# Two FFN pairs by seven block products, with the sums on VectorE, and transposes moved from TensorE to DMAs

## The chip, the cores and the metric

The kernel runs on one core of a Trainium2 chip. The core has five engines with a queue of instructions each: TensorE (PE in the profile; PEld is its weight load), VectorE (DVE), ScalarE (ACT), GpSimd (POOL) and SyncE (SP, which here only issues DMAs). They run side by side and meet at semaphores. The metric is the device time of one execution in microseconds (us); less is better.

## The reference, cut to what matters

It is one layer of a decoder, on 256 tokens of width 1024:

```
h    = rmsnorm(x);  u = h @ W_in        # columns: rnn_x | rnn_gate | q | k | v | two gates
A    = gelu(rnn_gate) * rg_lru(causal_dwconv4(rnn_x))
B    = causal attention of q, k, v      # 8 heads x 128; q and k normalised per head
y    = sigmoid(g_A) * (A @ P_A) + sigmoid(g_B) * (B @ P_B)
x    = x + y @ W_out
h    = rmsnorm(x)
x    = x + (gelu(causal_dwconv3(h @ W_up)) * (h @ W_gate)) @ W_down     # 2816 channels
```

Everything is fp32.

## The kernel before, in words

**Tiles and splits.** An fp32 product is made of three matmuls of fp32r operands (`mm3`): high by high, high by low, low by high, where high is the operand rounded to fp32r and low the rest. Weights come in chunks of 128x2048 (1 MB), each by one DMA of SP's queue into a tile `raw`; ScalarE makes `hi` by a cast, VectorE makes `lo` by a subtraction (`split_part`), and TensorE reads both. There are three `raw`, four `hi`, three `lo`. Activations are split by `split2` in the same way. TensorE's results go to eight PSUM banks, four in pool A and four in pool B.

**Units.** A unit of TensorE works off one or two chunks: `rx` (rnn_x), `rg` (rnn_gate), `k`, `q`, `v`, `ri` (the LRU's two small products), `ga` and `gb` (gates), `pr` and `pa` (P_A and P_B), `yo` (W_out), and in the FFN `up` and `gt` for five pairs of chunks (512 channels each, pairs 0 to 4), `last` for the eleventh chunk, and eleven `dn` (W_down, all added up in four banks `acc`). A unit of one chunk is 24 matmuls of 128x512. Between the units stand the heads' small products: scores `s`, transposed probabilities `pt`, outputs `o`.

**Turns.** A result that stands by tokens and is wanted by channels is turned by `turn`: a stream transpose of 32x32 blocks by VectorE, four DMAs to DRAM that reorder the blocks, one DMA back. TensorE transposes (three a head in `att_t`, 16 in `m_t` for the gated sum, 16 for `h2`) do the same through PSUM.

**FFN.** For each pair, `pair_up` copies the turned `up` into order (2 copies by VectorE), does the three-tap convolution (`conv3`: for each of four blocks one ScalarE activation and two VectorE multiply-adds of 128x255 and 128x254), then gelu; `pair_gate` multiplies with the turned `gt` and splits into `fah` and `fal`, which `dn` reads.

**LRU.** `lru_a` to `lru_d`, for each half of the channels: a product by VectorE (`rt` times the decay), tanh, exp and square of 128x1024 by ScalarE, a square root with its own ScalarE table, products and a scan by VectorE.

**The order.** Nothing is scheduled on the chip: the operations are recorded (all at line 296, `Later`), and `ORDER`, a table of numbers, says in which order they are issued. An engine works through its own row in that order. `preload_act_table(AF.Exp)` is such an operation: it loads a ScalarE table early.

Of the kernel before, what the change touches and what calls it, by code (L numbers as in the profile page):

```python
# [32 lines left out]
KEPT = {"upd": 2, "gtd": 2, "u": 1, "c": 2, "ah": 3, "al": 3, "s": 1}
UNITS = ("rx0 rx1 rx2 rx3 rg0 rg1 rg2 rg3 k0 k1 k2 k3 ri0 q0 q1 ri1 ga0 ga1 q2 q3 v0 v1 ga2 ga3 v2 v3 gb0 "
         "gb1 gb2 gb3 pr0 pr1 pr2 pr3 pa0 pa1 pa2 pa3")
AFTER = {
    "rx0.0": "s4 stats",
    "rg0.0": "ev0",
    "rg0.3": "ev1",
    "rg1.1": "rx0",  # L40
    "rg1.2": "s5 rx1",
    "rg1.3": "s6 ge0",
    "rg2.1": "xo0",
    "rg3.0": "rgr0",
    "rg3.1": "conv0",
    "rg3.2": "xo1",
    "rg3.3": "s7 ge1",
    "k0.0": "s8 s9",
    "k0.2": "rgr1 conv1",
    "k1.2": "s10 s11",  # L50
    "k1.3": "s12",
    "k2.2": "s13",
    "k2.3": "split0 decay",
    "k3.0": "gelu1 conv2 conv3 split1",
    "k3.3": "s14",
    "ri0.0": "s15",
    "ri0.2": "krs0 ks0",
    "q0.3": "krs1",
    "q1.2": "ks1",
    "q1.3": "s16 rk1",  # L60
    "ri1.3": "rk0",
    "ga0.1": "rq0",
    "ga1.1": "s17 Tk0",
    "q2.0": "s18",
    "q3.0": "s19",
    "q3.2": "Tq0",
    "v0.0": "s20",
    "v1.0": "Tk1",
    "v1.1": "qrs0",
    "v1.2": "S3 s21",  # L70
    "ga2.0": "S2",
    "ga2.1": "rq1 S1 Tq1",
    "ga2.2": "s22 S0 P3",
    "ga2.3": "s23",
    "ga3.0": "s24 s25 la0 la1",
    "ga3.1": "lb1",
    "ga3.2": "lc1 P1 lb0",
    "ga3.3": "s26",
    "v2.1": "P0 qrs1 S4",
    "v2.2": "O3 s27 s28",  # L80
    "v2.3": "ld1",
    "v3.2": "S5",
    "gb0.0": "P2",
    "gb0.1": "s29",
    "gb1.0": "gelu0 P4",
    "gb1.3": "s30 S6",
    "gb2.1": "S7",
    "gb2.2": "O2 lc0",
    "gb2.3": "O1 s31 s32 ld0",
    "gb3.0": "ya0",  # L90
    "gb3.1": "P5 ys0",
    "gb3.2": "O4",
    "pr0.0": "P7 sb0 s33",
    "pr0.2": "sa1 ya1",
    "pr0.3": "ys1",
    "pr1.0": "O5",
    "pr1.1": "s34",
    "pr1.2": "sa0",
    "pr1.3": "s35",
    "pr2.0": "P6",  # L100
    "pr2.1": "s36",
    "pr2.2": "O6",
    "pr2.3": "O0",
    "pr3.0": "s37",
    "pr3.3": "sb1",
    "pa1.0": "O7",
    "pa2.1": "m0",
    "pa3.2": "s38",
    "wo.0": "s39 m1",
    "wo.4": "m2",  # L110
    "wo.5": "s40",
    "wo.6": "m3",
    "wo.12": "n00",
    "wo.13": "n10",
    "wo.14": "s41",
    "up00.0": "s42 n01",
    "up00.2": "n11",
    "gt00.0": "s43",
    "gt00.3": "s44",
    "up01.0": "stats2",  # L120
    "up01.3": "s45 s46",
    "gt01.2": "s47",
    "up10.0": "ur0 s48",
    "up10.1": "s49",
    "up11.0": "s50",
    "up11.2": "fu0",
    "gt10.0": "s51",
    "gt10.1": "s52 gr0",
    "gt11.1": "ur1",
    "gt11.2": "s53",  # L130
    "up20.1": "fg0",
    "up21.1": "gr1",
    "up21.3": "s54",
    "gt20.2": "fu1",
    "gt21.0": "s55",
    "dn0.0": "fg1",
    "dn1.1": "gr2",
    "dn1.3": "s56",
    "up30.3": "s57 s58",
    "up31.0": "s59",  # L140
    "up31.3": "s60 ur2",
    "gt31.1": "ur3 s61",
    "gt31.2": "fu2",
    "gt31.3": "fu3 s62",
    "dn2.2": "fg2 s63 s64",
    "dn3.0": "s65",
    "up40.0": "gr3",
    "up41.3": "s66",
# [1041 lines left out]
```

## Time and profile before

| | us |
|---|---|
| median of three runs (433.44 to 434.73) | 434.29 |
| profiled execution, first to last instruction | 432.3 |
| TensorE busy in it | 427.6 (99%) |
| VectorE busy | 324.5 (75%) |
| ScalarE busy | 271.2 (63%) |
| TensorE's granted clock | 1.000 |

The profiled execution is known by its span alone; the median of the runs is 2.0 us above it, which is what lies around the first and the last instruction. Busy time of one instruction includes the overlap with the next one: where durations are added up, the distance from start to start is used, and it is read from the timeline. A matmul of 128x512 is shown with some 0.39 us, but the next one starts 0.227 us later.

### The profile page before, as it was taken

How to read it: one execution, taken by the hardware profiler on the slowest of the kernel's cores; microseconds unless marked ns; L12 is line 12 of the kernel's file. 1: busy time of each engine (PE TensorE's matmuls, PEld its weight loads, DVE VectorE, ACT ScalarE, POOL GpSimd, SP SyncE). 2: the span in 40 equal slices, each digit the busy share in tenths (PEclk: the TensorE clock that was granted, in tenths of full speed). 3: DMA queues.
4: the chain of work that ended last, by engine and by line, in shares of the span. 5: the costliest groups of instructions: out<-in, count | busy, mean ns of one | idle time of the engine just before them, and what ended most of it. 6: DMA issues, size and time to landing. Idle time of an engine off the chain costs nothing.

```text
span 432.3 us, 5409 instructions
## 1 busy us (share of the span) xinstructions
PE 427.6 (99%) x1992; PEld 357.3 (83%) x1992; DVE 324.5 (75%) x417; ACT 271.2 (63%) x307; POOL 51.9 (12%) x101
## 2 busy tenths in 40 slices
PE   9999999999999999999999999999999999999996
PEld 8888888888887888888888888888888888888885
DVE  4867499899898999865666796587888667769633
ACT  5687596886999998853241364468566556456510
POOL 0022483567160000000000000000000000000000
PEclk9999999999999999999999999999999999999999
DMA  7997945999991844474453556898888688788402
GB/s 253 395 394 256 339 169 149 295 314 335 368 313 38 284 142 149 130 238 134 181 194 116 176 203 207 299 325 253 284 265 313 237 270 262 243 286 293 152 0 97
DMA packets 33833, 101.09 MB, mean 234 GB/s; under 512 B 3216, under 2 KB 14096, under 8 KB 30352
## 3 DMA queue, kind: packets, MB, share of 16 engines
...
q10 hardware_dynamic: 144, 0.00, 0.0%
...
## 4 chain that ended last, share of the span: by engine, by line
PE 87%; DMA 5%; ACT 3%; DVE 2%; issue 2%; SPq 0%; ACTq 0%; DVEq 0%
PE acc L296 14%; PE up L296 13%; PE gt L296 13%; PE rx L296 5%; PE gb L296 5%; PE pr L296 5%; PE yo L296 5%; PE pa L296 5%; PE k L296 5%; PE rg L296 5%; DMA qm<-qd 3%; PE q L296 3%; PE last L296 3%; PE v L296 2%; DMA raw<-in_win_fm 2%
## 5 line engine op out<-in xcount | busy, mean ns | idle before, releaser
L296 DVE TENSOR_TENSOR lo<-raw,hi 128x2048 fp32r<-128x2048 f32 (+1 forms) x72 | 160.3, 2227 | 40.1 <-PE gt L296 10.5
L296 ACT CAST hi<-raw 128x2048 fp32r<-128x2048 f32 (+1 forms) x69 | 128.3, 1862 | 49.7 <-PE gt L296 11.8
L296 PE MATMUL up<-hi,h2h 128*128 128x512 f32 x80 | 31.3, 391 | 0.0
L296 PE MATMUL up<-hi,h2l 128*128 128x512 f32 x80 | 31.2, 389 | 0.0
L296 PE MATMUL up<-lo,h2h 128*128 128x512 f32 x80 | 31.1, 389 | 0.0
L296 PE MATMUL gt<-hi,h2h 128*128 128x512 f32 x80 | 31.1, 389 | 0.0
L296 PE MATMUL gt<-lo,h2h 128*128 128x512 f32 x80 | 31.1, 389 | 0.0
L296 PE MATMUL gt<-hi,h2l 128*128 128x512 f32 x80 | 31.1, 389 | 0.0
L296 PE MATMUL acc<-hi,fah 128*128 128x512 f32 x80 | 31.1, 389 | 0.0
L296 PE MATMUL acc<-lo,fah 128*128 128x512 f32 x80 | 31.1, 389 | 0.0
L296 PE MATMUL acc<-hi,fal 128*128 128x512 f32 x80 | 31.1, 389 | 0.0
L296 POOL TENSOR_TENSOR rsq<-rsq 128x8 f32<-128x8 f32 x32 | 19.2, 600 | 28.6 <-DVE rsq L296 26.3
L296 ACT ACT_TABLE_LOAD x15 | 19.2, 1283 | 1.4 <-PEq L1180 1.2
L296 DVE SCALAR_TENSOR_TENSOR fc<-fu,pv,fc 128x255 f32<-128x255 f32 (+1 forms) x40 | 17.3, 477 | 2.1 <-ACT fc L296 2.1
L296 ACT ACTIVATE fc<-fu,pv 128x256 f32<-128x256 f32 x20 | 10.8, 593 | 11.1 <-DVE fu L296 11.1
L296 PEld LDWEIGHTS up<-hi,h2l 128*128 128x128 f32 x80 | 15.0, 188 | 3.2
L296 PEld LDWEIGHTS acc<-lo,fah 128*128 128x128 f32 x80 | 15.0, 188 | 3.1
L296 PEld LDWEIGHTS acc<-hi,fal 128*128 128x128 f32 x80 | 15.0, 188 | 3.1
L296 PEld LDWEIGHTS gt<-hi,h2l 128*128 128x128 f32 x80 | 15.0, 188 | 3.1
L296 PEld LDWEIGHTS gt<-lo,h2h 128*128 128x128 f32 x80 | 15.0, 188 | 3.1
L296 PEld LDWEIGHTS gt<-hi,h2h 128*128 128x128 f32 x80 | 15.0, 188 | 3.1
L296 PEld LDWEIGHTS acc<-hi,fah 128*128 128x128 f32 x80 | 15.0, 188 | 3.1
...
## 6 DMA issues: line engine op xcount, KB each, us to landing
...
```

What stands on the lines that cost most here:

```text
L296: getattr(engine, name)(*map(real, a), **{n: real(v) for n, v in k.items()})
```

## The change

- **Pairs 2 and 4** (`ffn_group`, `group`). The four products of a pair (two halves of the tokens, two of the outputs: up and gate, each over two halves of the 1024 inputs) are a 2x2 block product. It is computed with seven block products in place of eight, of 12 matmuls each. The four weight tiles are called `x`, `y`, `w`, `z`; VectorE adds them up in place (`SUMS = "vvvv"`) to the operands `t1`, `t2`, `t4`, `t3`, and `b00`, `b10`, `b11` are split as they are. Four sums of `h` (`forms`: `R1`, `S2`, `S3`, `S4`) are the other operands. The outputs `fs0` and `fs1` are put together from the banks `a`, `b`, `c`, `d` by ScalarE and VectorE.
- **Probabilities** are turned by VectorE and DMAs (`turn` with three blocks; four writes of 48 KB, one read a head), not by TensorE.
- **Half the gated sum** (`MT = {0: True}`) goes by `turn`, the other half stays on TensorE.
- **FFN taps** (`taps`): twelve ScalarE activations a pair that read the turned tile directly, and two VectorE additions of 4x255 and 4x254.
- **LRU**: the decay is folded into tanh and exp as a per-channel scale (8 of 128x256 a half in place of 2 of 128x1024 and a VectorE product).
- **Buffers**: `raw` 5, `hi` 4, `lo` 4, 19 half tiles in place of 23, all eight banks in one pool; the residual is written to DRAM after the second norm and loaded again at the end. Three casts that VectorE did go back to ScalarE.
- **The order** is a new table.

```diff
-HALVES, SMALLS, WARM, RAWS = 23, 10, 11, 3
-DVE_HI = (39, 42, 43)
+HALVES, SMALLS, WARM = 19, 10, 11
+BUFS = {"raw": 5, "hi": 4, "lo": 4}
+SUMS = "vvvv"
+OPTS = "cdy"
+PLAN = """
+rx rg0 rg1 rg2 rg3 decay k0 k1 k2 k3 q0 q1 q2 q3 ri0 v0 v1:3 S3 P3 v1 ga0:1 S2 P2 ga0:1 S1 P1 ga0:1 S0 P0 ga0 ri1 ga1 v2:2 S4 P4 v2 v3:2 S5 P5 v3 O3 ga2:2 O2 ga2 ga3:1 S6 P6 ga3 gb0:1 S7 P7 gb0:1 O1 gb0 O0 gb1 O4 gb2 gb3 ya0 ya1 pr0 pr1:1 O5 pr1 pr2:2 O6
...
 ORDER = """
-0-2 +1 3-4 +1 5 +1 6 +1 8 +1 7 +1 9 +1 11 +2 10 25 +1 12 30 +1 26-27 +1 14 +1 28 33 +1 29 +1 13 31 +2 32 +2 34 +2
...
+0 2 1 3 +3 5 +4 6 +3 7 +1 8 10 9 11-13 15 14 132 18 24 17 29 26 25 28 +1 27 +3 32 30 +3 31 +2 33 +8 34 +7 36 35 +2 38
...
     def att_t(h):
-        sm = heads[h]
-        ps = bank(f"pt{h}")
...
+        turn(f"pm{h}", small(f"pd{h}", 384), probs[h], 3, probs[h])
+        a = small(f"ph{h}", 384, F32R), small(f"pl{h}", 384, F32R)
+        split2(*a, probs[h])
...
+    def group(name, a, src, rs, nrs, out0, out1, cols=True):
...
+        product(ps["a"], a["a00"], part("b00", x), True)
+        nc.scalar.activation(o[1][0], ps["a"], AF.Copy, scale=r[0])
+        nc.scalar.activation(o[0][1], ps["a"], AF.Copy, scale=r[1])
+        yield
+        add("1", x, y, src[0][1])
+        product(ps["c"], a["R1"], part("t1", x), True)
+        nc.scalar.activation(o[1][1], ps["c"], AF.Copy, scale=nrs[:, 1:2])
+        yield
+        product(ps["a"], a["a01"], part("b10", w), False)
+        nc.scalar.activation(o[0][0], ps["a"], AF.Copy, scale=r[0])
+        yield
+        product(ps["c"], a["S4"], part("b11", z), False)
+        yield
+        ps["b"] = bank(f"{name}b")
+        add("2", x, z, src[1][1])
+        product(ps["b"], a["S2"], part("t2", x), True)
+        nc.vector.scalar_tensor_tensor(o[1][0], ps["b"], r[0], o[1][0], op0=OP.mult, op1=OP.add)
+        nc.vector.scalar_tensor_tensor(o[1][0], ps["c"], nrs[:, 0:1], o[1][0], op0=OP.mult, op1=OP.subtract)
+        yield
+        ps["d"] = bank(f"{name}d")
+        add("4", w, x, None)
+        product(ps["d"], a["a11"], part("t4", w), True)
...
+            add("3", y, z, src[1][1])
+        product(ps["b"], a["S3"], part("t3", y), False)
+        nc.vector.scalar_tensor_tensor(o[0][1], ps["b"], r[1], o[0][1], op0=OP.mult, op1=OP.add)
+        nc.vector.tensor_sub(o[1][1], o[1][1], o[0][1])
+        nc.vector.scalar_tensor_tensor(o[0][1], ps["d"], r[1], o[0][1], op0=OP.mult, op1=OP.add)
...
+    MT = {0: True, 1: False}
...
+            turn(f"mm{g}", d, sgb.half(g))
...
+    def taps(c, d, m, n):
+
+        part = {k: half(f"w{k}{m}")[:, :n * S] for k in (1, 0)}
+        for i in range(n):
...
+            nc.scalar.activation(v(c), channels(d, i), AF.Identity, scale=w(2), bias=pv[:, V_FB + m + i:V_FB + m + i + 1])
+            for k in (1, 0):
+                nc.scalar.activation(v(part[k]), channels(d, i), AF.Copy, scale=w(k))
+        for k in (1, 0):
+            e = 2 - k
+            o = kt(c)[:, :, e:]
+            nc.vector.tensor_add(o, o, kt(part[k])[:, :, :S - e])
```

**Three places in the order.** The first is the start of ScalarE's row, which makes the first scaled input `xgh` from `xT` and the norm's factors `g`. In brackets stands what a row waits for; `DMAHW0` is here the DMA of `g`, `DMAHW1` that of `xT`. Before:

```order
L296 DMA g1_77<-in_vec 128x8
L296 ACT_TABLE_LOAD
L296 ACTIVATE xgh0_106<-xT0_81,g1_77 128x256 [waits DMAHW1_49,DMAHW0_49]
L296 ACTIVATE xgh0_106<-xT0_81,g1_77 128x256
L296 CAST his0_113<-raws0_85 128x512 [waits DMAHW3_49]
```

And now:

```order
L180 DMA g1_74<-in_vec 128x8
L180 ACT_TABLE_LOAD [waits DMAHW1_49]
L180 ACTIVATE xgh0_115<-xT0_76,g1_74 128x256 [waits DMAHW0_49]
L180 ACTIVATE xgh0_115<-xT0_76,g1_74 128x256
L180 CAST his0_122<-raws0_80 128x512 [waits DMAHW3_49]
```

The table load still stands ahead of `xgh`, but it now waits for `xT`: the new table issues the preload in the FFN (beside `dn5`), and the load that stands here belongs to the first activation and has taken over one of its waits.

The second place is the middle of the attention, while TensorE works on `ga3` and `gb0`. On ScalarE, `sm` are the heads' softmax, `tt`, `rt` and `a` belong to the LRU, `vh` is the high part of v, `ph` that of the probabilities. ScalarE's row now, from the second sigmoid table to the LRU's square root:

```order
L180 ACT_TABLE_LOAD
L180 ACTIVATE sm_1326,mx_1327<-sm_1326,mx_1327,rq_1048 128x128
L180 CAST higb_1419<-rawgb_1118 128x2048
L180 ACTIVATE tt_1446<-rt_949,ndec 128x256 x4
L180 ACTIVATE rt_949<-rt_949,cdec 128x256 x4
L180 ACTIVATE a_1479<-rt_949 128x1024
L180 ACTIVATE sm_1398,mx_1399<-sm_1398,mx_1399,rq_1048 128x128
L180 CAST higb_1490<-rawgb_1156 128x2048
L180 ACTIVATE vh_1501<-v_1285,rs_325 128x512
L180 CAST ph_1511<-sm_1150 128x384
L180 ACTIVATE vh_1501<-v_1291,rs_325 128x512
L180 ACT_TABLE_LOAD
```

Right behind it stands the square root of `tt`. VectorE's row there, where `it` times `tt` reads that square root and `vl` is the low part of v, made from the bank that holds `v_1285`:

```order
L180 SCALAR_TENSOR_TENSOR mx_1523<-mx_1523,rq_1048 128x2
L180 TENSOR_TENSOR pl_1533<-sm_1150,ph_1511 128x384
L180 TENSOR_TENSOR it_978<-it_978,tt_1446 128x1024
L180 SCALAR_TENSOR_TENSOR vl_1547<-v_1285,rs_325,vh_1501 128x512
L180 SCALAR_TENSOR_TENSOR vl_1547<-v_1291,rs_325,vh_1501 128x512
```

Here `vl` stands right behind that product. In VectorE's row of before it stands behind the LRU's scan, and the product some dozen rows further ahead:

```order
L296 SCALAR_TENSOR_TENSOR it_764<-rt_720,it_764 128x256 x3
L296 SCALAR_TENSOR_TENSOR vl_1558<-v_1380,rs_333,vh_1502 128x512
L296 SCALAR_TENSOR_TENSOR vl_1558<-v_1386,rs_333,vh_1502 128x512
L296 TENSOR_TENSOR lo_1567<-raw_1438,hi_1516 128x2048
L296 TENSOR_TENSOR ptl_1587<-pt_1569,pth_1576 128x384
```

The product that waits for the square root has moved to right ahead of `vl`, and TensorE's scores `s7` take the bank of `v_1285`, so they wait for that `vl`.

The third place is VectorE's row while TensorE works on pair 2. Before, with the splits of the weights, the taps of pairs 0 and 1 and two turns:

```order
L296 TENSOR_TENSOR lo_2555<-raw_2454,hi_2516 128x2048
L296 SCALAR_TENSOR_TENSOR fc_2543<-fu_2533,pv,fc_2543 128x255 x3
L296 SCALAR_TENSOR_TENSOR fc_2543<-fu_2533,pv,fc_2543 128x254 x4
L296 TENSOR_TENSOR lo_2595<-raw_2490,hi_2558 128x2048
L296 STREAM_TRANSPOSE fgtd_2612<-fs_2391 128x8x4x32
L296 COPY fu_2533<-fupd_2524 128x4x128 x2
L296 TENSOR_TENSOR lo_2640<-raw_2527,hi_2604 128x2048
L296 TENSOR_TENSOR fc_2543<-fgtd_2451,fc_2543 128x4x128 x2
```

And now:

```order
L180 TENSOR_TENSOR rawf2x<-rawf2x,rawf2z 128x2048
L180 TENSOR_TENSOR fc_2573<-fc_2573,w_2568 128x4x255
L180 TENSOR_TENSOR lof2b_2638<-rawf2w,hif2b_2624 128x2048
L180 TENSOR_TENSOR rawf2w<-rawf2w,rawf2x 128x2048
L180 TENSOR_TENSOR fc_2573<-fc_2573,w_2579 128x4x254
L180 TENSOR_TENSOR lof2t_2675<-rawf2x,hif2t_2661 128x2048
L180 STREAM_TRANSPOSE fupd_2693<-fs_2635 128x8x4x32
L180 TENSOR_TENSOR lof2b_2707<-rawf2z,hif2b_2689 128x2048
L180 STREAM_TRANSPOSE fgtd_2723<-fs_2655 128x8x4x32
L180 TENSOR_TENSOR fc_2573<-fs_2490,fc_2573 128x4x128 x2
L180 TENSOR_TENSOR lof2t_2749<-rawf2w,hif2t_2729 128x2048
L180 TENSOR_TENSOR lof2t_2763<-rawf2y,hif2t_2745 128x2048
```

Additions of whole weight tiles have come in between the splits, the copies are gone, and the product of pair 0's gate (`fc` with `fs`, which a turn brings) stands ahead of the last two splits of the group.

## Rows read from the trace of the kernel before

**Rows 1.** The page: busy time, share of the span and number of instructions of three engines, and the chain that ended last, by engine.

```profile
PE 427.6 (99%) x1992; PEld 357.3 (83%) x1992; DVE 324.5 (75%) x417; ACT 271.2 (63%) x307; POOL 51.9 (12%) x101
PE 87%; DMA 5%; ACT 3%; DVE 2%; issue 2%; SPq 0%; ACTq 0%; DVEq 0%
```

**Rows 2.** The chain that ended last, in order of time, its long pieces: start, length, what (x matmuls).

```profile
6.09 22.67 PE rx L296 x108
...
292.95 10.88 PE up L296 x48
303.83 10.88 PE gt L296 x48
...
358.23 10.88 PE up L296 x48
369.11 10.88 PE gt L296 x48
```

**Rows 3.** The same chain between 55 and 176 us: `ri`, a head's scores, outputs and transposed probabilities.

```profile
72.28 2.87 PE ri L296 x24
...
141.93 0.64 PE o L296 x6
...
148.09 0.70 PE s L296 x6
...
151.52 0.33 PE pt L296 x3
```

**Rows 4.** The same chain between 216 and 262 us: one of the four transposes of the gated sum.

```profile
225.67 0.44 PE mT L296 x4
```

**Rows 5.** Timeline of ScalarE from 0 to 6 us: start, length, instruction, idle time before it and what ended it.

```profile
1.15 1.28 ACT L296 ACT_TABLE_LOAD   x1 [1.15 <-PEq L1180]
4.16 0.91 ACT L296 ACTIVATE xgh<-xT,g 128x256 fp32r<-128x256 f32 x2 [1.73 <-DMA g<-in_vec]
```

**Rows 6.** Timeline of VectorE from 0 to 7.5 us.

```profile
4.89 0.29 DVE L296 CAST his<-raws 128x256 fp32r<-128x256 f32 x1 [3.91 <-DMA raws<-in_win_fm]
5.10 0.48 DVE L296 SCALAR_TENSOR_TENSOR xgl<-xT,g,xgh 128x256 fp32r<-128x256 f32 x1
5.50 0.42 DVE L296 TENSOR_TENSOR los<-raws,his 128x256 fp32r<-128x256 f32 x1
```

**Rows 7.** Timeline of TensorE from 5.5 to 7 us: the first matmuls of `rx`.

```profile
5.75 0.77 PE L296 MATMUL rx<-his,xgh 128*128 128x256 f32 x2
```

**Rows 8.** The instructions of the tile `xT`: its four DMAs, which SP issues from 0.7 us on, and their time from issue to landing.

```profile
L296 SPq DMA_DIRECT2D xT<-in_xT x4: 340/444/534, 0.7 to 8.0; - x4
...
DMA to landing us min/median/max: 3.3/7.9/9.6
```

**Rows 9.** Groups of instructions by line and form: count, busy time, mean ns of one, idle time before them.

```profile
L296 DVE TENSOR_TENSOR lo<-raw,hi 128x2048 fp32r<-128x2048 f32 x68 | 155.5, 2287 | 38.8 <-PE gt L296 10.5 <-issue 9.1 <-PE rg L296 7.0
L296 ACT CAST hi<-raw 128x2048 fp32r<-128x2048 f32 x65 | 124.2, 1912 | 48.0 <-PE gt L296 11.8 <-PE pr L296 6.5 <-PE pa L296 5.7
...
L296 ACT ACT_TABLE_LOAD x15 | 19.2, 1283 | 1.4 <-PEq L1180 1.2
...
L296 DVE STREAM_TRANSPOSE fupd<-fs 128x1024 f32<-128x1024 f32 x5 | 6.2, 1241 | 0.5 <-ACT fs L296 0.5
...
L296 DVE TENSOR_TENSOR lo<-raw,hi 128x1024 fp32r<-128x1024 f32 x4 | 4.8, 1222 | 1.3 <-ACT hi L296 1.2
...
L296 ACT ACTIVATE rt<-ri,pv 128x256 f32<-128x256 f32 x8 | 3.9, 482 | 0.0
...
L296 DVE SCALAR_TENSOR_TENSOR vl<-v,rs,vh 128x512 fp32r<-128x512 f32 x4 | 2.8, 747 | 0.1
```

**Rows 10.** Timeline of ScalarE in the attention, 118 to 155 us.

```profile
126.37 1.90 ACT L296 CAST hi<-raw 128x2048 fp32r<-128x2048 f32 x1
128.29 1.28 ACT L296 ACT_TABLE_LOAD   x1
129.58 1.07 ACT L296 ACTIVATE tt<-tt 128x1024 f32<-128x1024 f32 x1
130.66 1.28 ACT L296 ACT_TABLE_LOAD   x1
131.95 0.49 ACT L296 ACTIVATE sm<-sm,mx,rq 128x128 f32<-128x128 f32 x1
...
133.98 0.46 ACT L296 CAST pth<-pt 128x384 fp32r<-128x384 f32 x1
```

**Rows 11.** Busy time of each engine between 120 and 150 us: stretch, length, busy (x instructions) of PE, PEld, DVE, ACT, POOL, granted clock, DMA share, GB/s.

```profile
120.00:150.00 30.00, 29.62 (x156) 24.90 (x155) 26.38 (x62) 29.45 (x44) 6.84 (x13) 1.00 0.63 214
```

**Rows 12.** The same for three stretches of the FFN: pair 1, pair 2, and the first two `dn`.

```profile
271.19:292.95 21.76, 21.76 (x97) 18.02 (x97) 15.37 (x17) 12.12 (x13) 0.00 (x0) 1.00 0.93 310
292.95:314.71 21.76, 21.76 (x97) 18.02 (x97) 17.86 (x20) 16.26 (x17) 0.00 (x0) 1.00 0.84 262
314.71:325.59 10.88, 10.88 (x49) 9.01 (x49) 9.60 (x12) 7.50 (x9) 0.00 (x0) 1.00 0.87 278
```

**Rows 13.** Waits: who waited for whom, us in total, times, the longest.

```profile
DVE fu L296 <- DMA fupd<-upm: 5.6, 3, 2.0
...
DVE fc L296 <- DMA fgtd<-gtm: 3.0, 1, 3.0
```

**Rows 14.** DMAs: packets by size, and issues with KB each and the median us from issue to landing.

```profile
DMA packets 33833, 101.09 MB, mean 234 GB/s; under 512 B 3216, under 2 KB 14096, under 8 KB 30352
...
qm<-qd SPq DMA_DIRECT2D x8, 128.0 KB, 6.7
km<-kd SPq DMA_DIRECT2D x8, 128.0 KB, 7.7
qd<-qm SPq DMA_DIRECT2D x2, 512.0 KB, 6.1
kd<-km SPq DMA_DIRECT2D x2, 512.0 KB, 8.2
```

More of the change, by code (lines that the diff above doesn't have):

```diff
@@ L28 @@
 V_N = 170
-HALVES, SMALLS, WARM, RAWS = 23, 10, 11, 3
-AHEAD_S, AHEAD_L = 2, 3
-DVE_HI = (39, 42, 43)
[L33 to L148, printed above, removed]
-    "gt41.1": "s67 s68",
-    "gt41.3": "ur4",
-    "dn4.0": "fu4 s69",
-    "dn4.1": "s70 fg3",
-    "dn5.2": "lr5 gr4",
-    "dn5.3": "s71",
-    "dn7.0": "fu fg fg4",
-    "dn8.0": "s73",
-    "dn9.3": "s74",
-}
@@ L489, in trunk_layer @@
     sraw, shi, slo = pieces("raw"), pieces("hi", F32R), pieces("lo", F32R)
-    ptr["load"] = ptr["split"] = START
-    xs = const.tile([P, 2, D], F32, name="xs")
+    xe = [half(f"xe{t}") for t in range(2)]
     def load_x(a, b):
@@ new lines, in unit @@
+    def unit(kind, c):
+        if kind == "ri":
+            w = chunk(kind, c, 1024)
+            for n4 in range(4):
+                ri(c, w, n4)
+                if n4 == 3:
+                    lru(c)
+                yield
+            return
+        w = chunk(kind, c)
+        g, kh = c // 2, c % 2
+        if not kh:
+            open_ps[kind] = [bank(f"{kind}{g}{t}") for t in range(2)]
+        ps = open_ps[kind]
+        for k4 in range(4):
+            tm_mm(ps, w, 4 * kh + k4, k4, *{"pr": (yah, yal), "pa": (ybh, ybl)}.get(kind, (xgh, xgl)),
+                  kind not in "qkv")
+            if kh and k4 == 3:
+                evac[kind](g, ps)
+            yield
@@ new lines, in x_forms, with rg_group @@
+    def x_forms():
+        m = {}
+        for t in range(2):
+            for kh in range(2):
+                v = m[t, kh] = small(f"xf{t}{kh}", 512)
+                nc.vector.tensor_mul(v.rearrange("p (k t) -> p k t", t=P), kt(xTs.half(kh))[:, :, t * P:(t + 1) * P],
+                                     g1[:, 4 * kh:4 * kh + 4, None].to_broadcast([P, 4, P]))
+        return forms("xf", xgh, xgl, m, lambda n: small(n, 512, F32R))
+    xf = []
+    def rg_group():
+        if not xf:
+            xf.extend((x_forms(), negative(rs1, "nrs1")))
+        s = [half(f"gs{g}") for g in range(2)]
+        src = [[source["rg"](2 * g + kh) for g in range(2)] for kh in range(2)]
+        yield from group("rg", xf[0], src, rs1, xf[1], *s)
+        for g in range(2):
+            rg_turn(g, s[g])
@@ L969, in wo, with unspill @@
+    def unspill():
+        if "y" in OPTS:
+            for t in range(2):
+                xs[t] = half(f"xo{t}")
+                nc.sync.dma_start(xs[t], mid[t])
     def wo(j, t, hf):
[L970 removed]
+        if not xs:
+            load_res()
+        if j not in wos:
+            wos[j] = chunk("wo", j)
         if j == 0:
[L972 to L973 removed]
@@ L1125, in trunk_layer @@
+    NP = NF // 2
+    for token in PLAN.split():
+        step(token)
     with tc.manual_schedule():
```

641 lines of the change are left out of this document (330 added, 311 removed), and 84 rows, old and new, of the table ORDER.

## The prediction

> **What bounds the kernel now.** I read the page first. TensorE is busy for 427.6 of 432.3 us and makes up 87% of the chain that ended last; VectorE is busy for three quarters, ScalarE for 63% [rows 1]. The chain in order of time then shows that TensorE's matmuls follow one another without a gap almost from the start to the end: a unit of 48 matmuls takes 10.88 us, 0.2267 each, everywhere in the FFN [rows 2]. So the kernel is bound by the number of TensorE's columns, and work taken from TensorE is time gained as long as the others keep up. Whether they can is not told by the shares of the span: between 120 and 150 us ScalarE is busy for 29.45 of 30 us and VectorE for 26.38 [rows 11], while in pair 1 of the FFN VectorE has 15.37 of 21.76 [rows 12]. The attention is where the others are near to being the bound already. Of the waits, the ones for turned tiles tell how late a turn can be [rows 13].
>
> **What the change takes from TensorE.** Pairs 2 and 4 go from 96 matmuls to 84 each: 24 x 0.2267 = 5.44 us [rows 2]. Eight heads lose their three transposes, 8 x 0.33 = 2.64 [rows 3]. Half of the gated sum loses 2 x 0.44 = 0.88 [rows 4]. Together **-8.96 us**, if TensorE stays dense. All of it lies on the path now.
>
> **What it adds at the start: +0.8.** Before, ScalarE's table load stands without a wait at 1.15 to 2.43 and is hidden by the DMAs; `xgh` begins at 4.16, when `g` has landed [rows 5], VectorE casts the first weights at 4.89 before it comes to `xgl` and `los` [rows 6], and the first `rx` matmul starts at 5.75, right behind the warming matmuls [rows 7]. Now the load waits for `xT`, which is issued at 0.7 and lands 3.3 us later at the earliest, at some 4.0 [rows 8]. With 1.29 from load to next instruction [rows 10] `xgh` begins at about 5.3, 1.2 later. VectorE's row now has `xgl` first, so it waits for that too: `xgl` at 5.85, the casts behind it at 6.25 and 6.45, the first `rx` matmul at 6.5. That is 0.8 later, and nothing behind it makes it up, since TensorE is dense. Bounds: 0, if `xT` lands early and the load hides, and 1.3, the whole load.
>
> **What it adds in the attention: +2.8.** TensorE's scores `s7` now take the bank of `v_1285`, which VectorE's `vl` has to read first, and that `vl` stands behind a product that waits for ScalarE's square root. From the end of `s4` to the start of `s7` TensorE has half of unit v2, then v3, ga2, ga3 and a quarter of gb0 (90 matmuls, 20.4 us) with two heads' scores and outputs between them (2 x 0.70 + 2 x 0.64 [rows 3]), 23.1 us. On the other side stands one row: VectorE's maxima of `s4`, about 1.0; ScalarE's instructions from the exponential of `sm4` to the square root, which are three exponentials (1.6), three table loads at 1.29 (3.9; one for the sigmoids, one back, one for the root), four sigmoids and eight tanh and exp of 128x256 at 0.41 from start to start (4.9), three casts of probabilities (1.1), four activations of 128x512 (2.3), two casts of weights at 1.81 (3.6), the square and the root (1.9) [rows 9, 10]; that is 19.3; then VectorE's product 1.2 and `vl` 0.75 [rows 9]. Together 22.3, just within 23.1, if VectorE takes up `s4` at once. It doesn't: added up from the end of unit k1, VectorE's row to that maximum holds 66.5 us (ten splits of weights at 2.2, the conv's 24 multiply-adds at 0.4 to 0.5, ten stream transposes, products of the LRU, the heads' softmax steps) and begins 2.7 late, since the first split waits for ScalarE's cast; TensorE's row to the same point holds 65.9. VectorE is 3.3 behind, so `s7` starts 22.3 + 3.3 - 23.1 = 2.5 late; the bank of `s6` for the second half of gb0's first quarter costs a part of it earlier, and with it the sum is 2.8. Bounds: 0 if the lag is not there (22.3 is below 23.1); above, all that the change adds to a ScalarE that is full in this stretch [rows 11], 16 activations at 0.41 for 4 at 1.0 (2.6), and the 2.6 of transposes that no longer cover it: 5.2. I take the count.
>
> The Trainium skill, ScalarE: Activation LUTs, section What ACT_TABLE_LOAD costs, says that a switch of tables costs 1.28 us and a drain of 1.38 besides, 2.66 in all. The trace agrees with the load and not with the drain: the instruction behind a load starts 1.29 after it [rows 10]. By the page the three loads of this row would be 4.1 more.
>
> **What it adds in the FFN: +0.5, and three small places: +1.2.** In a group VectorE has seven splits and four sums of 128x2048, 11 x 2.2 = 24.2 us [rows 9], where TensorE has seven products, 84 x 0.2267 = 19.0. A sum is taken at a split's price: the same operation on the same shape. To that come five combinations of 128x512 at 0.66, two turns at 1.17, two tap sums at 1.14, a gate's product 1.2 and a split of 1.14: 34.5. A plain pair has four splits 8.8, turns 2.3, tap sums 2.3, gate 1.2 and last split 1.1: 15.7. Taken over pair 0 to pair 3 (two plain pairs, the group, two `dn` and a plain pair), with some 5 for the second norm's `h` and 5 for its forms, VectorE has 3 x 15.7 + 5 + 5 + 34.5 + 4.4 = 96 us, TensorE 21.76 x 3 + 19.0 + 10.9 = 95.2. VectorE is full, with nothing to spare; but it begins with tiles ahead (five `raw`), and gates and `fal` may slip until `dn` reads them, so the row closes nearly without a stall. What it lacks is patience: pair 0's gate product, which waits for a turn's DMA, stands ahead of the last two splits of the group. Before, VectorE waited up to 3.0 for such a tile once, and up to 2.0 for the copies, which ScalarE's taps have taken over [rows 13]. I take 0.5, bounds 0 and 6 (a wait of 3.0 in each group). The small places, counted in the same way: the split of ya0 ahead of pr0 0.4, the second norm's forms ahead of up01 0.5, and `dn6`, whose taps meet the displaced preload and the load back to gelu (2 x 1.29 on ScalarE, most of it hidden), 0.3. Bounds 0 and 2.
>
> **At no cost.** ScalarE's taps, 12 x 0.45 a pair, go where it had 12.12 of 21.76 busy [rows 12]. Spilling and loading the residual is four DMAs of 512 KB, and nothing waits for them until the last additions. POOL's additions are three small ones. The probabilities' turns replace a TensorE transpose by a stay in DRAM: in the order some 16 us lie between the transpose of a head and the cast that reads it back, and a turn of 128 KB pieces takes 6.7 + 6.1 (q) to 7.7 + 8.2 (k) [rows 14]: hidden, the second by a hair.
>
> **The sum**, against the profiled execution: 432.3 - 8.96 + 0.8 + 2.8 + 0.5 + 1.2 = 428.6; with the 2.0 around the span **430.6 us**, against a median of 434.3.
>
> **The rivals.**
>
> *TensorE stays dense.* The lag in the attention and the FFN's waits vanish, the start's 0.8 and half of the small places remain: 432.3 - 8.96 + 0.8 + 0.6 + 2.0 = 426.7. For it speaks that a count of instructions can't see a row that is a little faster; against it that VectorE and ScalarE are full exactly where work is added [rows 11]. Chance 0.18.
>
> *The groups are bound by VectorE.* Place: VectorE's row in G2 and G4. If a turned tile comes 3 us late in each group, and splits, sums and gates can't slip past, the two stalls are 6 us, with lateness of pair 3's gate some 8: 430.6 + 5.5 = 436 to 438. Slower than before from 3.7 us of such stalls on. For it: 96 against 95.2 us, and the 3.0 and 2.0 seen in waits [rows 13]; against it: those waits stood in a row with slack. Chance 0.17.
>
> *The probabilities come late.* Place: ScalarE's casts `ph`, which stand in the very row that leads to `s7`. Their writes have pieces of 384 bytes where the turns of before have 1024; before, 3216 of 33833 packets are under 512 bytes, and 4096 such are added [rows 14]. If a turn takes 21 us where 16 are there, ScalarE's row is 5 late and so is `s7`: 435.6; with 8 late 438. Slower from about 3.7 us of lateness on. The Trainium skill, DMA: Bandwidth & Descriptors, section Specifications, gives 512 bytes as the least for full rate and a read-modify-write below; no row here shows what such a turn takes. Chance 0.12.
>
> *The drain is real.* If each of the three loads on the row to `s7` held its successor back as long as the load itself again, 3 x 1.29 = 3.9: 434.5. Rows speak against it [rows 10]. Chance 0.03.
>
> *The clock falls after a pause.* The granted clock is 1.00, its higher level, in all stretches that I read [rows 11, 12], and TensorE hardly pauses there. With a pause of 2 us before `s7` it might fall; at half clock some microseconds of matmuls would take twice as long: 433 to 435. Chance 0.05.
>
> **How the numbers follow.** The forecast has 0.45, from 428.5 to 433. What a measurement of this kernel can tell from no change is about 0.3%, 1.3 us: faster is under 433.0, slower over 435.6. Faster: the dense case, the forecast, and 0.04 of the others, 0.67. Same: half of the drain and clock cases, the mild ends of both late cases, 0.13. Slower: the rest of the late cases, 0.20. The range from 425.5 to 437 leaves out the better half of the dense case's low end and the worst of the two late ones.
>
> **What would show it.** The first `rx` matmul at about 6.5, with the table load ending near 5.3; TensorE idle for 2 to 3 us before `s7`, VectorE as the one waited for, and behind it the square root; VectorE above 95% busy from `gt1` to `gt3` and TensorE with gaps under 1 us there; TensorE's busy time near 418.6. The forecast is wrong if TensorE's gaps in the groups exceed 3 us in sum, or if ScalarE waits for `sm` DMAs ahead of `ph`.

## The result and the profile after

The kernel after the change takes 429.69 us (429.29 to 430.29, four runs) against 434.21 on the same chip: a ratio of 0.9894 [0.9878, 0.991] (in brackets, here and below, the 95% interval). Times are medians; one run of e12, 525.84 us at a granted clock of 0.755, is left out of its median. The profiled execution spans 428.2 us where before had 432.3. Its page, against [rows 1] and [rows 14]:

```profile
PE 420.2 (98%) x1936; PEld 348.1 (81%) x1936; DVE 356.1 (83%) x409; ACT 310.5 (72%) x377; POOL 53.6 (13%) x102
PE 68%; DVE 11%; ACT 7%; POOL 5%; DMA 4%; issue 3%; SPq 1%; ACTq 0%; DVEq 0%
DMA packets 41179, 108.45 MB, mean 253 GB/s; under 512 B 8128, under 2 KB 20544, under 8 KB 37696
```

TensorE still bounds the kernel, but the chain has less of it (68% for 87%): at several places the chain now runs through another engine. TensorE's waits, in us in total, times, and the longest:

```profile
PE s L180 <- DVE vl L180: 1.5, 1, 1.5
PE rx L180 <- DVE his L180: 1.2, 1, 1.2
```

The start. ScalarE's timeline, against [rows 5]:

```profile
4.06 1.28 ACT L180 ACT_TABLE_LOAD   x1 [4.06 <-DMA xT<-in_xT]
5.35 0.91 ACT L180 ACTIVATE xgh<-xT,g 128x256 fp32r<-128x256 f32 x2
...
9.16 1.05 ACT L180 CAST his<-raws 128x1024 fp32r<-128x1024 f32 x1 [2.39 <-DMA raws<-in_win_fm]
```

and TensorE's, against [rows 7]:

```profile
6.73 0.48 PE L180 MATMUL rx<-his,xgh 128*128 128x256 f32 x2 [1.23 <-DVE his L180]
...
10.26 0.73 PE L180 MATMUL rx<-his,xgh 128*128 128x512 f32 x2 [0.42 <-ACT his L180]
```

The load waits for `xT` as predicted, and the first `rx` matmul starts 0.98 later. A second pause follows at 10.26: the third piece of weights lands late. (What the start costs is not settled by this one profile; see e9.)

The attention. VectorE's timeline from the maximum of `s4` to TensorE's scores `s7`, which start at 154.14:

```profile
131.29 0.42 DVE L180 CUSTOM_DVE_ANT_0 sm<-s,mask 128x256 f32<-128x256 f32 x1
...
148.14 2.29 DVE L180 TENSOR_TENSOR logb<-rawgb,higb 128x2048 fp32r<-128x2048 f32 x1 [1.05 <-ACT higb L180]
...
152.07 1.23 DVE L180 TENSOR_TENSOR it<-it,tt 128x1024 f32<-128x1024 f32 x1 [0.41 <-ACT tt L180]
153.34 1.41 DVE L180 SCALAR_TENSOR_TENSOR vl<-v,rs,vh 128x512 fp32r<-128x512 f32 x2
```

and the two ends of ScalarE's row there, between which it never waits:

```profile
132.29 0.60 ACT L180 ACTIVATE sm<-sm,mx,rq 128x256 f32<-128x256 f32 x1 [1.33 <-DVE mx L180]
...
150.98 1.06 ACT L180 ACTIVATE tt<-tt 128x1024 f32<-128x1024 f32 x1
```

The product `it` waits for the root `tt`, and `vl` stands behind it. But VectorE waits only 0.41 there: its own row is almost as late as the root. That row had itself waited for a cast of ScalarE's, 1.05 at 148.14.

The FFN's first group in the chain that ended last, against [rows 2]:

```profile
292.81 2.73 PE f2a L180 x12
295.54 2.80 PE f2c L180 x12
298.33 2.76 PE f2a L180 x12
301.09 2.80 PE f2c L180 x12
303.89 2.80 PE f2b L180 x12
...
309.46 2.80 PE f2b L180 x12
```

Seven products stand back to back. At 0.2267 a matmul each would take 2.72. Windows over that stretch and the first `dn` behind it (columns as in [rows 11]):

```profile
293.00:314.00 21.00, 21.00 (x93) 17.01 (x92) 20.87 (x14) 19.14 (x16) 0.00 (x0) 1.00 0.73 251
314.00:326.00 12.00, 12.00 (x55) 9.94 (x54) 11.93 (x11) 10.57 (x15) 0.00 (x0) 1.00 1.02 388
```

VectorE is full for 33 us (its busy time follows those of PE and PEld) and TensorE doesn't wait. The probabilities' turns, by DMA issues, KB each and us to landing:

```profile
pm<-pd SPq DMA_DIRECT2D x32, 48.0 KB, 2.7
sm<-pm SPq DMA_DIRECT2D x8, 192.0 KB, 5.9
```

Every term can be measured the same way: a unit's time is the distance from its first matmul's start to the next unit's, read from TensorE's timeline of both kernels and added up over the units of one name.

| term | predicted | measured |
|---|---|---|
| matmuls of pairs 2 and 4 | -5.44 | -4.64 (192 in 43.52; now 168 in 38.88) |
| transposes of P and of half the gated sum | -3.52 | -3.57 (`pt` 2.17, gaps behind it in `v` 0.57, `mT` 0.70, `yo` 0.13) |
| start | +0.8 | +1.48 (first `rx` 0.98, `rx` itself 0.50) |
| `s7` | +2.8 | +1.29 (`gb` 22.42, now 23.71; the pause is 1.64) |
| `pr0` | +0.4 | +0.14 (with `pa`) |
| groups, `up01`, `dn` | +1.3 | +1.09 (`up` and `gt` 0.62, `dn` 0.47) |
| sum | -3.7 | -4.2; the last matmul ends 4.30 earlier |

### The profile page after: what moved, and what is told of

It is laid out like the page before. It is cut to its first block, busy times and chain, and to the rows that moved or that the text cites. A ratio compares the mean times of both kernels' runs of the same rounds, so it can differ in the third digit from the quotient of the medians.

```text
span 428.2 us, 5443 instructions
## 1 busy us (share of the span) xinstructions
PE 420.2 (98%) x1936; PEld 348.1 (81%) x1936; DVE 356.1 (83%) x409; ACT 310.5 (72%) x377; POOL 53.6 (13%) x102
## 2 busy tenths in 40 slices
DMA packets 41179, 108.45 MB, mean 253 GB/s; under 512 B 8128, under 2 KB 20544, under 8 KB 37696
## 4 chain that ended last, share of the span: by engine, by line
PE 68%; DVE 11%; ACT 7%; POOL 5%; DMA 4%; issue 3%; SPq 1%; ACTq 0%; DVEq 0%
PE acc L180 12%; PE up L180 8%; PE gt L180 8%; PE pa L180 5%; PE yo L180 5%; PE pr L180 5%; PE rg L180 5%; PE rx L180 4%; POOL rsq L180 3%; PE last L180 3%; PE k L180 2%; DMA raws<-in_win_fm 2%; DVE lov L180 2%; SPq L180 1%; PE f4b L180 1%
## 5 line engine op out<-in xcount | busy, mean ns | idle before, releaser
L180 PE MATMUL acc<-lodn,fah 128*128 128x512 f32 x80 | 31.2, 390 | 0.1
L180 PE MATMUL acc<-hidn,fah 128*128 128x512 f32 x80 | 31.2, 390 | 0.0
L180 PE MATMUL acc<-hidn,fal 128*128 128x512 f32 x80 | 31.2, 389 | 0.0
L180 DVE TENSOR_TENSOR lodn<-rawdn,hidn 128x2048 fp32r<-128x2048 f32 x11 | 25.0, 2281 | 0.9 <-ACT hidn L180 0.8
L180 ACT CAST hidn<-rawdn 128x2048 fp32r<-128x2048 f32 x11 | 21.0, 1908 | 0.4 <-PE f4c L180 0.2
L180 ACT ACTIVATE w<-fs,pv 128x256 f32<-128x256 f32 x44 | 19.6, 498 | 0.5 <-DMA fs<-upm 0.5
L180 PE MATMUL up<-hiup,h2h 128*128 128x512 f32 x48 | 19.0, 396 | 0.0
L180 PE MATMUL up<-hiup,h2l 128*128 128x512 f32 x48 | 18.8, 392 | 0.0
L180 PE MATMUL gt<-higt,h2h 128*128 128x512 f32 x48 | 18.7, 389 | 0.0
L180 PE MATMUL gt<-higt,h2l 128*128 128x512 f32 x48 | 18.7, 389 | 0.0
```

The source lines that it names most:

```text
L180: getattr(engine, name)(*map(real, a), **{n: real(v) for n, v in k.items()})
```

## Experiments

All kernels start from the kernel after the change. `MOVES` takes one recorded operation out of the order and puts it ahead of another; numbers are those of the order's table. e1, e2 and so on are the experiments' labels. Ratios are against the kernel before on the same chip, which took 434.21 to 434.59 us on the chips used. A unit's time or a wait is read from one profile of each kernel.

**e1: The preload moved back to the start.** 4 is the preload of Exp's table, 24 the first `xgh`.

```diff
+MOVES = ((4, 24),)
```

> The changed kernel with one operation moved: the preload of the exponential table is issued at the start, ahead of the first scaled input, as before the change, and no longer beside dn5. Theory 1 (TensorE is dense and each of its late starts is paid in full): the table load ends before xT lands, xgh starts near 4.2 in place of 5.35, the first rx matmul near 5.6 to 5.8 in place of 6.73, and the end of rx moves by 1.0 to 1.5 us: 428.2 to 428.7 against 429.7. In the FFN two table loads of ScalarE (2.6 us) ahead of pair 3's gelu go too, which TensorE doesn't see. Rival (the start is bound by the weights' DMAs, and the table load is hidden): the first matmul moves, but the end of rx stays at 30.2 and the time at 429.7.

Measured: 429.16 us (428.78 to 429.57), 0.988 [0.9862, 0.9898]; between the two theories, and not told apart from 0.9894. The first `rx` matmul is back at 5.66, but unit `rx` takes 23.93 in place of 23.35. The load was hidden again, and the third weights' DMA took half of it back.

**e9: The whole start in before's manner**: also the DMAs of weights pieces ahead of the second and third of `xT`, VectorE's first casts ahead of `xgl`, and the split of a later piece ahead of the next inputs.

```diff
+MOVES = ((4, 24), (8, 7), (9, 10), (25, 26), (27, 28), (40, 36), (41, 37))
```

> The changed kernel with its start put back to that of before in three ways: the table's preload first, the first weights cast ahead of xgl, and the first pieces of rnn_x's weights issued ahead of the second and third pieces of xT. Moving the preload alone brought the first matmul from 6.73 to 5.66, but rx ended only 0.5 us earlier, since TensorE then waited 1.2 us for ScalarE's cast of the third piece of the weights, whose DMA landed at 8.9 where it had landed at 7.9 before the change. Theory 1 (that piece is late because the new order issues pieces of xT among the weights): it lands near 8, rx ends at 27.6 to 27.9 as before, and the time is 428.2 to 428.5. Rival (the landing times at the start differ from run to run by themselves): the time stays at 429.0 to 429.3, and the wait at rx is the same.

Measured: 428.91 (428.76 to 429.72), 0.9876 [0.9856, 0.9895], between the two theories again. ScalarE's timeline of it:

```profile
1.17 1.28 ACT L189 ACT_TABLE_LOAD   x1 [1.17 <-PEq L1176]
4.23 0.91 ACT L189 ACTIVATE xgh<-xT,g 128x256 fp32r<-128x256 f32 x2 [1.78 <-DMA g<-in_vec]
...
7.59 1.05 ACT L189 CAST his<-raws 128x1024 fp32r<-128x1024 f32 x1 [1.01 <-DMA raws<-in_win_fm]
```

How much of this is the order can be read only across profiles. The time to the end of `rx` (start of the first matmul plus the unit) is 28.60 before. In the ten profiles here that keep the changed start it is 28.76 to 30.56, median 29.6; in the two with before's order (this one and e13) it is 28.79 and 28.42. So the start costs about 1.0 in the middle and scatters by 1.8.

Two things scatter. The first large cast begins between 7.22 and 9.16, with the landing of its DMA. And TensorE's clock rises at another moment in each profile. In e4 the large cast comes earliest of all, and yet `rx` ends second to last, at 30.34. ScalarE's cast and TensorE's matmuls there:

```profile
7.22 1.04 ACT L189 CAST his<-raws 128x1024 fp32r<-128x1024 f32 x1 [0.45 <-DMA raws<-in_win_fm]
```

```profile
9.86 0.63 PE L189 MATMUL rx<-his,xgl 128*128 128x256 f32 x2
10.28 0.44 PE L189 MATMUL rx<-los,xgh 128*128 128x256 f32 x2
10.56 0.40 PE L189 MATMUL rx<-his,xgh 128*128 128x256 f32 x2
```

Up to 10.4 a matmul of 128x256 starts 0.21 after the last, behind it 0.12: the lower of the clock's two levels (1.2 GHz) and then the higher (2.4 GHz). In e4 and e3 (30.56) the first 17 matmuls of `rx` run at the lower level, some 1.7 us each time. Before has seven of them, up to 7.2, which cost it 0.74; the other eight profiles of the changed start, the kernel after among them, have none. Among those that have none a later large cast mostly goes with a later end, from 7.32 and 28.76 (e10) to 9.16 and 30.08 (after). The 1.48 of the one profile is 0.98 for the later first matmul, -0.74 for the clock and 1.24 for more waits; it is not a fixed price, and e1's half gain lies within the scatter.

**e2: `vl` ahead of the product that waits for the root.** 530 and 532 are the two `vl`, 375 the product. The tiles this needs are found by one half tile more and one small tile fewer.

```diff
-HALVES, SMALLS, WARM = 19, 10, 11
+HALVES, SMALLS, WARM = 20, 9, 11
+MOVES = ((530, 375), (532, 375))
```

> The changed kernel with VectorE's two vl of the second half of v issued ahead of the product it times tt, which waits for ScalarE's square root; for that vl has a buffer of its own (20 half tiles and 9 small ones in place of 19 and 10). Theory 1 (a single wait: s7 waits for the bank that vl reads, and vl stands behind that product): the pause of 1.5 to 1.6 us before s7 goes, and the time falls by 1.3 to 1.6 to some 428.2. Theory 2 (a backlog: VectorE and ScalarE have more work in the attention than TensorE, and the pause only shows where it comes out): the pause comes back in pieces at gb0 or at the next outputs o1 and o0, and the time stays between 429.3 and 430.8.

Measured: 431.95 (431.57 to 433.01), 0.9942 [0.9926, 0.9957]: slower by 2.3. TensorE's waits:

```profile
PE gb L189 <- DVE mx L189: 1.4, 1, 1.4
...
PE o L189 <- DVE ybl L189: 0.8, 1, 0.8
PE ga L189 <- ACT sga L189: 0.7, 1, 0.7
...
PE s L189 <- DVE vl L189: 0.6, 1, 0.6
PE pr L189 <- DVE yal L189: 0.4, 1, 0.4
```

The wait at `s7` goes from 1.5 to 0.6, and four others come. Neither theory's time is met. (The profiled run is the slowest of the six, 433.01; the others are 431.57 to 431.99.) But the kernel doesn't test the order alone. One of the new waits, for `sga` at 138.7, comes ahead of everything that was moved (150 us and later), and ScalarE's waits between 110 and 160 us tell why:

```profile
ACT ph L189 <- DMA pm<-pd: 3.3, 1, 3.3
```

ScalarE stands for 3.34 ahead of a `ph` at 138.70, until a probabilities' write from `pd` has landed; in the kernel after it doesn't wait there. The `sga` behind it starts at 139.12, where it starts at 136.19 in the kernel after. `pd`, `ph` and `pl` are small tiles, and this kernel has one fewer. So ScalarE's whole row is some 3 us late before the moved operations begin. Whether `vl` ahead of the product would help stays open.

**e11: No root table in the LRU's first half.** An exponential stands in the root's place, so two table loads go; this kernel leaves the root out.

```diff
-        nc.scalar.activation(t, t, AF.Sqrt)
+        nc.scalar.activation(t, t, AF.Exp if h == 0 else AF.Sqrt)
```

> The changed kernel with the exponential in place of the square root for the first half of the LRU (the root is left out, the numbers are others), so that ScalarE needs no table switch there: two loads, 2.6 us, less on its row, both right ahead of the product that vl stands behind. If it is the wait for the root that holds s7: the pause of 1.6 us goes, 428.0 to 428.4. If it is ScalarE's backlog further ahead (the casts vh, which stand ahead of the root, are late themselves): the pause before s7 shrinks only to 0.7 to 1.2, and what the root's loads held back behind it (gb0, pr0) gives some tenths more: 428.7 to 429.2.

Measured: 429.58 (428.01 to 429.66), 0.989 [0.9872, 0.9907]: neither of the times, and not told apart from the kernel after. The profiled run is the 428.01, the other three took 429.5 to 429.7; its `rx` ends at 28.97 where that of the kernel after ends at 30.08. VectorE's timeline:

```profile
150.49 1.22 DVE L189 TENSOR_TENSOR it<-it,tt 128x1024 f32<-128x1024 f32 x1
151.74 1.41 DVE L189 SCALAR_TENSOR_TENSOR vl<-v,rs,vh 128x512 fp32r<-128x512 f32 x2
```

The product waits for nothing now; the pause before `s7` falls from 1.64 to 1.14 only. So the root's lateness is worth 0.5 of it, and VectorE's own row the rest; that row waits 1.05 for ScalarE's cast `higb` ahead of it here too. The place is that of the second theory, ScalarE's backlog, though the time isn't. From the `vh` cast ahead of the load to the activation behind it lie 148.99 to 150.98 in the kernel after and 147.90 to 148.48 here: 1.99 against 0.58, so a load in front of an activation costs this row 1.41. The Trainium skill, ScalarE: Activation LUTs, section What ACT_TABLE_LOAD costs, has 1.28 and a drain of 1.38; the trace agrees with the first alone.

**e12: The LRU's decay by VectorE again**: 8 tanh and exp of 128x256 a half become 2 of 128x1024, and VectorE multiplies.

```diff
+MOVES = ((363, 477), (468, 598))
...
-        if "d" in OPTS:
+        if h not in (0, 1):
...
         else:
             nc.vector.tensor_mul(kt(a), kt(a), cdec[:, 4 * h:4 * h + 4, None].to_broadcast([P, 4, S]))
             nc.scalar.activation(t, a, AF.Tanh, scale=-1.0)
             nc.scalar.activation(a, a, AF.Exp)
```

> One part undone: the LRU's decay is multiplied by VectorE again (one product of 128x1024 a half, set ahead of the softmax of s4 and beside gb0), and tanh and exp are two activations of 128x1024 a half in place of eight of 128x256: 1.3 us less on ScalarE in each half, 1.1 more on VectorE. The root, its tables and the order around vl stay. If ScalarE's backlog sets the pauses: the pause before s7 and the one before pr0 shrink, 1.0 to 1.6 us less, 428.1 to 428.7. If VectorE's backlog sets them: 1 us more, 430.7. If it is the wait for the root alone: the same time, 429.7.

Measured: 428.42 in the middle of three runs (428.11 to 428.64), 0.9862 [0.9844, 0.9879]. Its pause at TensorE:

```profile
153.18 0.33 PE L192 MATMUL s<-kTh,qTh 128*128 128x128 f32 x1 [0.74 <-DVE vl L192]
```

`gb` falls from 23.71 to 22.97 and `pr` from 22.37 to 21.93; that is 1.2 of the 1.38 by which its last matmul ends earlier. The eight take 3.33 from start to start (141.44 to 144.77) in the kernel after, the two 2.18 here; VectorE's product takes 1.14, and VectorE had waited 0.62 for `a` and 1.05 for a cast of ScalarE's there. So that part of the change, by itself, cost some 1.2 us: the medians say 1.3, though the intervals of the two ratios still touch.

**e7: Transposes of P by TensorE again**, three a head, in place of stream transpose and five DMAs.

```diff
-        turn(f"pm{h}", small(f"pd{h}", 384), probs[h], 3, probs[h])
+        ps = bank(f"pt{h}")
+        for b in range(3):
+            nc.ops.append((nc.tensor.engine, "transpose", (ps[:, b * P:(b + 1) * P], probs[h][:, b * P:(b + 1) * P], ident), {}))
```

> One part undone: the probabilities are transposed by TensorE again (24 transposes), each set some 12 instructions ahead of ScalarE's cast, and VectorE's eight stream transposes and 40 DMAs go. Theory 1 (TensorE's count): 24 transposes cost 2.2 to 3.0 us, from which comes off what VectorE's lighter row gives back before s7 (8 x 0.5 us of work less, so the pause of 1.6 shrinks to 0.5): 430.5 to 431.5 against 429.7. Rival (turning by DMAs costs as much as it saves, by the backlog in the attention): 429.7 or less.

Measured: 431.69 (431.61 to 432.11), 0.9938 [0.9921, 0.9955], just above theory 1's range: the turns of the probabilities by DMA are worth 2.0. The 24 transposes take 1.98 again, and the pause moves: none at `s7`, and TensorE waits 1.6 for `ybl` ahead of an `o`. A pause of that size stays without the turns, so they alone are not its cause.

**e3: The groups' sums cut to 8 of 2048 columns** (the rest of each sum is left out).

```diff
-                nc.vector.tensor_add(to, to, tile_)
+                nc.vector.tensor_add(to[:, :8], to[:, :8], tile_[:, :8])
```

> The changed kernel with the eight sums of weight tiles by VectorE cut to 8 of 2048 columns (the rest of the sums is left out, so the products of pairs 2 and 4 are of other numbers): 8 x 2.2 = 17 us less work for VectorE. Theory 1 (TensorE's matmuls set the time in the groups, the sums are hidden): 429.7 within 0.5; a group still takes 19.4 us, unless its matmuls, which start 0.232 after one another where plain ones do at 0.227, are slowed by what VectorE does beside them: then 0.8 less. Rival (VectorE sets the time in the groups): TensorE's units around the groups close up and 3 us or more are gained.

Measured: 429.69 (428.94 to 430.55), 0.9893 [0.9872, 0.9913], and 19.44 and 19.42 for the groups, which take 19.44 with whole sums. Some 17 us of VectorE's work are hidden in full.

**e4: An eighth product**, the one with `t4` twice in each group.

```diff
+        product(ps["d"], a["a11"], t4, True)
```

> The changed kernel with one of the seven products done twice in each group (the product with a11 is started again in its bank, so the result is the same): 12 matmuls of 128x512 more a group, as many as the plain pair has, and nothing added for the other engines. Theory 1 (TensorE's count sets the time): 24 x 0.227 to 0.232 = 5.4 to 5.6 us more, 435.2. Rival (the groups are bound by VectorE, and TensorE waits there): under 2 us more.

Measured: 435.06 (434.12 to 435.76), 1.0014 [1.0002, 1.0026]: 5.4 more. The chain:

```profile
304.20 2.80 PE f2b L189 x12
307.00 5.49 PE f2d L189 x24
```

Each added product is paid for in full. With eight, nothing of the whole change is left: the gain hangs on those 24 matmuls.

**e5, e6: One split more in each group** (`t3`), and **four more** (`t1`, `t2`, `t4`, `t3`), each done twice.

```diff
+TWICE = (849, 970)
```

> The changed kernel with one split of each group (the low part of t3, 2.2 us on VectorE) done twice with the same result. If VectorE has no slack in the groups, as the sum 96 against 95 us said: a good part of 2 x 2.2 shows, 431.5 to 433.5. If VectorE is ahead by some microseconds there: under 0.5, 429.7 to 430.2.

Measured: 432.15 (432.08 to 432.24), 0.9947 [0.9928, 0.9965]. VectorE's timeline:

```profile
305.17 4.61 DVE L192 TENSOR_TENSOR lof2t<-rawf2y,hif2t 128x2048 fp32r<-128x2048 f32 x2
309.70 0.74 DVE L192 SCALAR_TENSOR_TENSOR fs<-f2b,rs,fs 128x512 f32<-128x512 f32 x1
```

TensorE's last product waits for that `fs`, which empties the bank `f2b`: G2 takes 21.27, 1.83 more. In the kernel after, the same `fs` ends at 307.84 + 0.74 = 308.58 and the product starts at 309.46: VectorE was 0.9 ahead. G4 stays at 19.44 and `dn` takes 0.8 more.

```diff
+TWICE = (832, 841, 849, 846, 953, 962, 970, 967)
```

> The same with four splits of each group (t1, t2, t4, t3) done twice, 8.8 us more on VectorE in each group, as if a sum cost twice its price. No slack: 12 to 17 us more, 442 to 447. Slack of some 4 us a group: 8 to 9 more, 438. Slack of a whole pair of chunks: under 3 more.

Measured: 444.71 (444.11 to 445.72), 1.0238 [1.0215, 1.0261]: 15.0 for some 17.6 us of splits. TensorE waits 4.3 for `lof2b` in G2 and 2.8 for `lof4b` in G4. Its timeline at the first wait, and windows behind both:

```profile
304.79 0.78 PE L192 MATMUL f2c<-lof2b,hfS4h 128*128 128x512 f32 x1 [4.28 <-DVE lof2b L192]
305.36 0.63 PE L192 MATMUL f2c<-hif2b,hfS4l 128*128 128x512 f32 x1
305.79 0.63 PE L192 MATMUL f2c<-hif2b,hfS4h 128*128 128x512 f32 x1
```

```profile
304.00:308.50 4.50, 3.71 (x9) 2.98 (x10) 4.50 (x5) 0.37 (x1) 0.00 (x0) 0.62 1.06 369
308.50:312.00 3.50, 3.50 (x16) 2.81 (x16) 3.47 (x3) 2.78 (x2) 0.00 (x0) 1.00 0.85 305
...
375.20:380.30 5.10, 5.05 (x15) 4.03 (x16) 5.07 (x3) 0.97 (x1) 0.00 (x0) 0.67 0.78 281
```

Behind each pause, at once or 1.3 us later, eight matmuls stand some 0.43 apart, not 0.23, and the granted clock is 0.62 and 0.67 over the windows: some 1.6 us each time. So of the 15.0 some 3.2 are the clock's, and 11.8 are left for the 17.6 of splits.

**e10: Plain blocks of `h` in place of its sums** as the groups' other operands (the values are other ones).

```diff
+        at.update(R1=at["a01"], S2=at["a00"], S3=at["a01"], S4=at["a10"])
```

> The changed kernel with the groups' products reading plain blocks of h as their stationary operand wherever they read one of the four forms (the forms are still made, but the products are of other numbers). In a group the matmuls with forms start 0.232 us after one another, those with the first block of h 0.227, as plain units do. Theory 1 (the operand tile decides: the forms stand in small tiles of their own): all of a group's products come to 0.227 to 0.228, a group to 19.1 in place of 19.44, and the time falls by 0.6. Rival (what runs beside a group, or its own order of banks, decides): the spacing stays at 0.232 for the second and later products, and the time at 429.7.

Measured: 429.29 (428.19 and 430.39), 0.9882 [0.9844, 0.9921]; the two runs say little, the chain more:

```profile
294.27 2.72 PE f2c L189 x12
296.99 2.72 PE f2a L189 x12
299.71 2.82 PE f2c L189 x12
302.53 2.72 PE f2b L189 x12
...
307.97 2.72 PE f2b L189 x12
```

Six of seven products are back at 2.72 and a group takes 19.14. So reading the sums of `h` costs 0.3 of the 0.4 us by which a group is longer than 84 x 0.2267 = 19.04. Whether their place in memory or their values do it stays open; products that read plain blocks (`f2a`, `f2d`) also got faster.

**e13: The better pieces together**: the start of e9, the decay of e12, and `dn5`'s split ahead of pair 4's first combination.

```diff
+MOVES = ((4, 24), (8, 7), (9, 10), (25, 26), (27, 28), (40, 36), (41, 37), (363, 477), (468, 598), (1010, 971))
```

> The changed kernel with the start of e9, the LRU of e12, and the split for dn5 ahead of the last combinations of pair 4. If the gains add up (0.8 for the start, 1.0 to 1.6 for the LRU, 0.3 for dn5): 427.0 to 427.7. If the start's gain is given back in the attention, where ScalarE is full whatever the start does: 428.0 to 428.5.

Measured: 428.23 (427.73 to 428.7), 0.9858 [0.9842, 0.9873], the lowest of all. It is 1.5 below the kernel after by medians, with intervals of the ratios that just part, and 0.2 below e12, which is not told apart. By units the start gives 1.66, `gb` and `pr` 0.97, and `dn` takes 0.55 back. Its chain towards the end:

```profile
405.14 1.23 DVE fal L192
...
406.42 14.79 PE acc L192 x64
```

TensorE now waits 0.6 for the last pair's `fal`, behind that pair's turn, ScalarE's taps and gelu. The kernel after has TensorE in that place for 25.84 us without a break. So what is gained ahead is in part given back here: 0.55 of 2.63. In e11's profile, which is 2.03 ahead, nothing is given back; whether the moved split for `dn5` has a share in it stays open. The time lies in the second range of what was expected, but not for its reason: the start's gain is kept through the attention.

## Why the prediction was right

**TensorE's count** was the right frame: e4 gets back 5.4 us for 24 matmuls, and e3 shows that the sums cost nothing. The term was mis-sized: 0.2267 a matmul [rows 2] was taken for matmuls that stand 0.2314 apart (19.44 / 84), 0.8 us in all; e10 shows most of it in the operands. TensorE's busy time is 420.2, 1.6 above the 418.6 foreseen.

**The transposes** gave 3.57 for 3.52. e7 gives 2.0 for P's alone.

**The start**: the mechanism up to the first matmul was as said: the load ends at 5.34 and the first matmul comes at 6.73 for 6.5. The step "nothing behind it makes it up, since TensorE is dense" was wrong. TensorE was not dense there before: its first seven `rx` matmuls ran at the lower clock (the two of [rows 7] take 0.77, the two in their place now 0.48), and that gives 0.74 back. Against it, the later weights pieces land late too, which was not in the sum, and in e3 and e4 the clock rises later still. Over ten profiles the start costs 0.16 to 1.96.

**The attention**: place, engine and chain were right, the size (2.8) was not: the pause is 1.64, and `gb` grows by 1.29. The count can be held against the trace piece by piece. From the end of `s4` (129.33) to `s7` TensorE has 23.17 without the pause, where 23.1 were counted. VectorE takes up the maximum of `s4` at 131.29, and from there the row to `s7` takes 22.85 (22.3 counted); ScalarE's part of it is 19.8 (19.3). The lag of VectorE, from 129.33 to 131.29, is 1.96 where 3.3 were counted: that is the mis-sized term, since 1.96 + 22.85 - 23.17 = 1.64. For the 0.3 of `s6`'s bank there is no wait. e11 shows that VectorE's own row, held up by the same ScalarE, would be only 0.5 sooner than the root, and e12 that the eight activations in place of two, which are in the count, make up 1.2 of what `gb` and `pr` cost.

**The groups**: "VectorE is full, with nothing to spare" was right within a microsecond: it is 0.9 ahead in G2 (e5), and of 17.6 us added some 11.8 show (e6, without the clock's share). "Above 95% from `gt1` to `gt3`" holds from 293 on (99%), not ahead of it, where the window from 272 has 18.55 of 21 us (88%).

**The rivals.** *Dense* falls with the pauses behind the start: 1.64 at `s7`, 0.23 at `pr0`, 0.36 in `up01` and 0.28 in `dn5`, 2.5 us in all, and with the start. *Bound by VectorE* falls by e3 and by TensorE's chain without a gap in the groups, though by 0.9 us only. *Late probabilities* falls: their writes landed in 2.7 and the reads in 5.9, 8.6 together where the order has some 16, with 8128 packets under 512 B, and ScalarE waits for none of them ahead of a `ph`. VectorE does wait 2.6 and 0.5 at 136 to 140 us for writes out of `pd`, but it makes that up: it waits for ScalarE again (0.62 and 1.05) ahead of `s7`. The Trainium skill, DMA: Bandwidth & Descriptors, section Specifications, asks for 512 bytes or more for full rate. No run here shows whether it matters: in the kernel after, writes of 48 KB land in 2.7, those of 128 KB in 2.4 to 7.3. *The drain* falls by e11: a load costs 1.41, not twice 1.29. *The clock* didn't fall here: it is 1.00 behind the 1.6 us pause (154 to 160 us).

The total was nearer (429.69 for 430.6) than its terms, and that is luck: start and operands came out 1.5 dearer, attention and small places 2.0 cheaper. What lies around the span is 1.8 in every run on record, not 2.0.
